# Seven block products over most of both wide layers' second matrix product, with weight sums made ahead in DRAM by adding transfers

## The chip, the core and the metric

One Trainium2 chip, one of its cores. The metric is device time of one execution in microseconds (us); lower is better. The kernel before ran three times at 1183.87, 1184.27 and 1186.08 us.

PE is the matrix engine (TensorE), PEld its weight loads, DVE VectorE, ACT ScalarE, POOL GpSimd, SP the engine that issues most transfers.

## The reference, cut to what matters

The input is 512 tokens of width 1024, float32. There are two layers. Each adds an attention part to the running sum `h` and then a wide layer (MLP) of width 4096:

```python
def sq_relu_mlp(h, w_up, w_down):
    u = jax.nn.relu(h @ w_up)
    return (u * u) @ w_down
...
    for layer in range(DEPTH):
        ...
        h = h + sq_relu_mlp(rmsnorm(h, norm_ffn[layer]), ffn_w_up[layer], ffn_w_down[layer])
    return rmsnorm(h, final_norm)
```

`w_up` is 1024x4096, `w_down` 4096x1024. The change is about the second product, `(u * u) @ w_down`, of both layers.

## The kernel before, in words

**Number format.** Every float32 operand is split into a high part (an ACT copy to float32r) and a low part (a DVE subtraction of the high part from the source); a product is three matrix instructions: high by high, high by low, low by high. Weights come in chunks: a transfer on SP's queue into a raw buffer, then the high part on ACT and the low part on DVE. `weights(i)` (L237) asks for the transfers of five chunks ahead and the splits of two chunks ahead; the split tiles `whi` and `wlo` have three buffers each.

**Plain products.** `product` (L415) with `mm3` (L500 to 503): for each 128 rows of the inner dimension and each 128 output columns, three matrix instructions over all 512 tokens, accumulating in a PSUM bank of its own; DVE adds the bank to `hT`, the running sum held transposed (L1265).

**Products with seven blocks.** `Seven` (L314) does a 2x2 block product (two 128-row blocks of the inner dimension, two 128-column blocks of the output, two halves of 256 tokens) with seven block products instead of eight. The sums of weight blocks are made after each load by three POOL instructions (`seven_chunk`, L302 to 304), the sums of token blocks by `sums` (L331). For 256 output columns `run` (L376) goes through all inner pairs, 21 matrix instructions over 256 tokens each (L388 to 390), and then combines the products in five ACT and DVE steps (L396 to 400).

**One wide layer**, `mlp` (L1250). The first product's first six tiles (of 128 columns of `u`) are made plainly (`plain`, L1160), the other 26 by `Seven`, two tiles in each of 13 runs of 84 matrix instructions. Each run squares its result (L1148, L1149) and either splits it into high and low parts (`pair_evac`) or keeps it raw (`raw_evac`). The second product is done in stages between those runs, as `SIZES` (L1108) says: layer 0 takes 6, 8 and 8 tiles of `u` plainly and 10 with `Seven`; layer 1 takes 6, 8 and 6 plainly, 8 with `Seven`, and 4 in a last product that puts tokens on the output's rows (`down`, L1621). While the last plain stage runs, `convert` (L1243) makes the token sums on DVE and splits them. Layer 0's second plain stage also carries the writing of the bias table for the next attention (`bias_rows`, L1215).

**Order of the work.** Each engine and each queue runs its own instructions in order; a scheduler orders them by readiness and program order, except where `keep_in_program_order` pins one and in the second attention, where the order is the written one (`fixed_order`, L957). 30 slots of 4 KB per partition (`Slot`) hold most intermediate tiles; they are handed out in rotation. A chunk of `Seven` takes a slot when more than `reserve` are free, else one of four `raw` buffers.

Attention comes first in each layer: layer 0 in `attend` (L961), where POOL scales each probability tile (L1005), layer 1 in `attend_C` (L1412; POOL at L1430), with plain products of later stages filled in (`Fill`, L471).

Of the kernel before, what the change touches and what calls it, by code (L numbers as in the profile page):

```python
# [16 lines left out]
S = 512  # L17
# [18 lines left out]
def encoder_kernel(ctx: ExitStack, tc: tile.TileContext, ins, out, dbg=None):  # L36
# [277 lines left out]
    class Seven:  # L314
# [61 lines left out]
        def run(self, ids, evac):  # L376
# [5 lines left out]
            for kp in range(self.np):  # L382
                hi, lo = weights(ids[kp])
                for n, ((a, b), (i, z)) in enumerate(zip(SEVEN, dst)):
# [5 lines left out]
                    PE.matmul(o, wl, x[:, 0], start=False, stop=kp == self.np - 1, skip_group_check=True)  # L390
                    yield 0.355
# [107 lines left out]

    def mm3(o, wh, wl, xh, xl, first, last):  # L500
        PE.matmul(o, wh, xh, start=first, stop=False)  # L501
        PE.matmul(o, wh, xl, start=False, stop=False)  # L502
        PE.matmul(o, wl, xh, start=False, stop=last)  # L503
# [271 lines left out]

    kst = Slot()
# [184 lines left out]
    def attend(heads, step):  # L961
# [46 lines left out]
        for h in heads:  # L1008
            for i in range(4):
                ripe = list(late_v)  # L1010
                p = scores(h, i)
# [77 lines left out]

    fill.add("z", product(w_in, 0, XP, tiles(768, 384), ev_cq, three))  # L1090
# [17 lines left out]
    SIZES = (6, 8, 8, 10), (6, 8, 6, 8, 4)  # L1108

    def first_product(l):  # L1110
# [10 lines left out]
        state = dict(c=SIZES[l][0], ids=None, plain=False, split=iter(()))  # L1121
# [68 lines left out]
        def stage(n, raw=0, more=0):  # L1190
# [4 lines left out]
            while left:  # L1195
                i = state["ids"]
                state["c"] += 2
                left -= 2
                if left:
                    ahead()  # L1200
                for _ in x7.run(i, raw_evac if more <= left < more + raw else pair_evac):
                    pass
# [12 lines left out]
    def bias_rows():  # L1215
        R, Fi, Fe = Slot(F32), Slot(F32), Slot(F32)
        rpb = ins["od_rpb"][0]
        for qr in range(8):
            SP.dma_start(R.t[16 * qr : 16 * qr + 16, 0:248],
                           rpb.rearrange("h a b -> h (a b)")[:, (7 - qr) * 31 : (7 - qr) * 31 + 248])  # L1220
# [9 lines left out]
        for c in range(16):  # L1230
            SP.dma_start(bxv[0, c].rearrange("r h k -> r h k"), Fi.t[:, (15 - c) * 8 : (15 - c) * 8 + 256])
# [3 lines left out]
            SP.dma_start(bxv[1, c][:, :, 128 * v : 128 * v + 128], Fe.t[:, off : off + 128])  # L1235
            yield
            SP.dma_start(bxv[1, c][:, :, 128 - 128 * v : 256 - 128 * v], Fe.t[:, 256:384])
# [5 lines left out]
    def convert(u7, R):  # L1243
        held = tc.keep_in_program_order
        for kp, raw in enumerate(R):
            yield from u7.sums(kp, raw, DVE, held)
            yield
            yield from u7.split(kp, held)

    def mlp(l, last=None):  # L1250

# [3 lines left out]
        beside = lambda m, i: None  # L1258
        k0 = 0
        for z, n in enumerate(SIZES[l][:3]):  # L1260
            U, R, V = stage(n, *(SIZES[l][3:] if z == 2 else ()))
            up = [s_.pair() for s_ in U]

            def ev(m, b):
                DVE.tensor_tensor(hT[:, m, :], hT[:, m, :], b, op=ALU.add)  # L1265

            gens = [product(w, k0, up, tiles(512 * c, 512), lambda j, b, c=c: ev(4 * c + j, b)) for c in range(2)]
            k0 += n
            work = iter(())
            if z == 2:  # L1270
                u7 = Seven(2 * len(R))
                ids = [u7.plan(w, 256 * m, k0) for m in range(4)]
                if last:
                    beside = last(k0 + 2 * len(R), V)
                reserve[0] = 8
                work = convert(u7, R)
            else:
                ahead()
            for c, gen in enumerate(gens):
                for i, _ in enumerate(gen):  # L1280
                    if z == 0:
                        later(c, i)
                    elif z == 1:
                        next(bias, None)
                    next(work, None)
            for _ in work:
# [442 lines left out]
```

## Time and profile before

| what | value |
|---|---|
| median of three runs | 1184.27 us |
| span of the profiled execution | 1184.0 us |
| PE matrix instructions | 7128, busy 98% of the span |
| DVE, ACT, POOL busy | 75%, 54%, 44% |
| bytes moved | 128.01 MB, mean 108 GB/s |

The page gives the profiled execution's span, from its first to its last instruction, and no other time of that execution; the median of the timed runs lies 0.27 us above it. Rows of a group of instructions give engine, operation, output and inputs, shape, count, busy time and mean duration, then the idle time of that engine just ahead of them and what ended it. Rows of a stretch give, for each engine, its busy time in that stretch and the number of instructions, then the granted PE clock, the DMA engines' busy share and GB/s. PE's busy time counts overlapping instructions as busy, so how fast PE goes is read from a stretch's length and its number of instructions.

### The profile page before, as it was taken

The page shows a single profiled execution, that of the slowest core. Times are in us where ns is not written, and L with a number is a line of the kernel's source. Part 1 is how long each engine was busy: PE and PEld are TensorE (multiplying, and loading weights), DVE is VectorE, ACT ScalarE, POOL GpSimd, SP SyncE. Part 2 cuts the span into 40 slices and gives each one's busy share as a digit, 9 for nine tenths or more (in the row PEclk, how much of TensorE's full clock was granted, in tenths as well). Part 3 has the DMA queues.
Part 4 walks back from the last instruction along what each step waited for, and adds up shares of the span by engine and source line. Part 5 has one row for each costly group of instructions (what it writes and reads, how often), then busy time and mean ns, then how long its engine had stood idle before and what let it go on. Part 6 is the DMA issues. An engine that isn't in the chain of part 4 may idle for free.

```text
span 1184.0 us, 19784 instructions
## 1 busy us (share of the span) xinstructions
PE 1160.5 (98%) x7128; PEld 1021.2 (86%) x7128; DVE 883.2 (75%) x1514; ACT 640.3 (54%) x1081; POOL 526.1 (44%) x662
## 2 busy tenths in 40 slices
PE   9989999999999999999999999999999999999997
PEld 8667778888899899988998998988889989998895
DVE  5788998878967368786884676667996736778975
ACT  4468676664546247562553565555554624666344
POOL 3267343224562377819602232231376625774710
PEclk9999999999999999999999999999999999999998
DMA  7223225212524723225226464433352341322412
GB/s 244 71 54 92 68 78 134 62 56 77 167 86 134 263 70 90 72 90 165 67 72 178 131 184 126 116 112 109 107 165 76 115 134 55 98 64 89 143 36 71
DMA packets 110145, 128.01 MB, mean 108 GB/s; under 512 B 9075, under 2 KB 86816, under 8 KB 110048
## 3 DMA queue, kind: packets, MB, share of 16 engines
q1 hardware_dynamic: 106992, 119.30, 33.5%
q0 software_dynamic: 2304, 6.31, 2.2%
q8 instruction: 56, 0.92, 0.3%
q10 hardware_dynamic: 752, 1.15, 0.3%
q14 instruction: 41, 0.34, 0.1%
HBM read 104.32 MB, written 6.29 MB: 93 GB/s over the span
## 4 chain that ended last, share of the span: by engine, by line
PE 81%; DVE 4%; ACT 1%; issue 1%; POOL 0%; DVEq 0%; ACTq 0%
PE mm L503 8%; PE mm L501 8%; PE mm L502 8%; PE mm L390 4%; PE mm L389 4%; PE mm L388 4%; PE t L388 3%; PE t L389 3%; PE t L390 3%; PE s L502 2%; PE s L503 2%; PE s L501 2%; PE s L390 2%; PE s L388 2%; PE s L389 2%; PE s L997 2%
## 5 line engine op out<-in xcount | busy, mean ns | idle before, releaser
L309 DVE TENSOR_TENSOR wlo<-a,whi 128x896 fp32r<-128x896 f32 x132 | 161.8, 1230 | 83.7 <-ACT whi L308 82.9
L308 ACT ACTIVATE whi<-a 128x896 fp32r<-128x896 f32 x132 | 125.0, 950 | 155.0 <-PE o L502 45.8
L501 PE MATMUL mm<-a,whi 128*128 128x512 f32 x485 | 195.9, 406 | 0.9 <-DVE a L915 0.7
L503 PE MATMUL mm<-a,wlo 128*128 128x512 f32 x485 | 192.1, 397 | 2.5 <-DVE wlo L202 2.5
L502 PE MATMUL mm<-a,whi 128*128 128x512 f32 x485 | 192.5, 397 | 0.1
L202 DVE TENSOR_TENSOR wlo<-raw,whi 128x1024 fp32r<-128x1024 f32 (+4 forms) x117 | 139.3, 1193 | 66.4 <-ACT whi L212 63.9
L212 ACT ACTIVATE whi<-raw 128x1024 fp32r<-128x1024 f32 (+3 forms) x120 | 116.4, 971 | 92.2 <-PE s L502 39.8
L302 POOL TENSOR_TENSOR a<-a 128x128 f32<-128x128 f32 x132 | 85.1, 645 | 173.3 <-DMA a<-in_ffn_w_up_dram 103.9
L303 POOL TENSOR_TENSOR a<-a 128x256 f32<-128x256 f32 x132 | 120.2, 910 | 10.3
L304 POOL TENSOR_TENSOR a<-a 128x128 f32<-128x128 f32 x132 | 115.1, 872 | 10.3
L503 PEld LDWEIGHTS mm<-a,wlo 128*128 128x128 f32 x485 | 91.7, 189 | 23.7 <-DVE wlo L202 3.4
L501 PEld LDWEIGHTS mm<-a,whi 128*128 128x128 f32 x485 | 91.8, 189 | 20.4 <-PE t L972 0.9
L502 PEld LDWEIGHTS mm<-a,whi 128*128 128x128 f32 x485 | 91.9, 190 | 17.4 <-DVE a L545 0.4
L388 PE MATMUL mm<-a,whi 128*128 128x256 f32 x370 | 103.9, 281 | 0.0
L389 PE MATMUL mm<-a,whi 128*128 128x256 f32 x370 | 103.9, 281 | 0.0
L390 PE MATMUL mm<-a,wlo 128*128 128x256 f32 x370 | 103.7, 280 | 0.0
L1005 POOL TENSOR_SCALAR p<-p,ti 128x512 f32<-128x512 f32 x64 | 46.2, 724 | 92.3 <-DVE ti L1004 81.1
L1430 POOL TENSOR_SCALAR p<-p,ti 128x256 f32<-128x256 f32 x64 | 35.6, 567 | 104.8 <-DVE ti L1429 91.8
L388 PE MATMUL t<-a,whi 128*128 128x256 f32 x264 | 74.2, 281 | 0.0
L389 PE MATMUL t<-a,whi 128*128 128x256 f32 x264 | 74.1, 281 | 0.0
L390 PE MATMUL t<-a,wlo 128*128 128x256 f32 x264 | 73.9, 280 | 0.0
L390 PEld LDWEIGHTS mm<-a,wlo 128*128 128x128 f32 x370 | 69.6, 188 | 0.2 <-DVE wlo L309 0.2
(338 smaller groups left out, 3210.8 us busy)
## 6 DMA issues: line engine op xcount, KB each, us to landing
a<-in_ffn_w_up_dram SPq DMA_DIRECT2D x104, 256.0 KB
raw<-in_ffn_w_down_dram SPq DMA_DIRECT2D x46, 512.0 KB
raw<-in_od_w_qkv_dram SPq DMA_DIRECT2D x64, 128.0 KB
a<-in_ffn_w_down_dram SPq DMA_DIRECT2D x28, 256.0 KB
raw<-in_ffn_w_up_dram SPq DMA_DIRECT2D x12, 512.0 KB
raw<-in_ev_w_in_dram SPq DMA_DIRECT2D x12, 384.0 KB
a<-a SPq DMA_DIRECT2D x18, 256.0 KB
bias<-bx SPq DMA_DIRECT2D x16, 256.0 KB
```

Source lines behind the costliest of these rows:

```text
L202: z = lambda: (eng or DVE).tensor_tensor(to, src, f32(high), op=ALU.subtract)
L212: ACT.activation(hi[:, 0:m], raw[:, 0:m], AF.Copy)
L303: POOL.tensor_tensor(r[:, 4:6], r[:, 2:3].to_broadcast([P, 2, P]), r[:, 0:7:6], op=ALU.add)
L304: POOL.tensor_tensor(r[:, 7], r[:, 3], r[:, 5], op=ALU.subtract)
L308: ACT.activation(hi[:, 0:896], raw[:, 128:1024], AF.Copy)
L309: DVE.tensor_tensor(lo[:, 0:896], raw[:, 128:1024], f32(hi[:, 0:896]), op=ALU.subtract)
L388: PE.matmul(o, wh, x[:, 0], start=kp == 0 and n in (0, 1, 3, 5), stop=False, skip_group_check=True)
L389: PE.matmul(o, wh, x[:, 1], start=False, stop=False, skip_group_check=True)
L390: PE.matmul(o, wl, x[:, 0], start=False, stop=kp == self.np - 1, skip_group_check=True)
L501: PE.matmul(o, wh, xh, start=first, stop=False)
L502: PE.matmul(o, wh, xl, start=False, stop=False)
L503: PE.matmul(o, wl, xh, start=False, stop=last)
```

## The change

- Layer 0's second product becomes 6 tiles of `u` plainly and 26 tiles (13 pairs) with seven block products; layer 1's becomes 6 plainly, 22 (11 pairs) with seven, and 4 in `down` as before. The 13 runs of the first product now follow one another, and their 26 tiles are all kept raw.
- The seven products use blocks of two 128-row blocks by two 512-column halves by two 256-token halves. The sums of weight blocks are made in DRAM, ahead of time: for each pair ACT issues two copies of 512 KB from `w_down` to a DRAM tile `made`, and POOL issues four transfers of 256 KB that add one block to another in DRAM. That makes 78 steps in layer 0 and 66 in layer 1. `tick` hands out one step for every 4.7 us (layer 0) or 5.5 us (layer 1) of counted PE work, from the start of the attention's filled products on; `drain` issues whatever is left before the sweeps.
- The products run in three sweeps over all pairs: two block products for each pair in the first sweep, two in the second, three in the third. A step loads its weights (512 KB, in the third sweep 768 KB) and splits them; the token sums and their splits are made one step ahead on DVE and ACT. Sums over products are partly left to PSUM: a bank goes on accumulating from one sweep into the next, and its content is added to or subtracted from `hT` in between. The last two pairs are done half by half of the output (`TAIL`).
- The bias table is written beside the second and third sweeps, and layer 1's first four groups of transposes of `hT` move from beside `Seven` into `down`.

```diff
+    def tick(us):
+        beat["left"] -= us
+        if beat["left"] <= 0:
+            beat["left"] += beat["every"]
+            next(beat["work"], None)
...
     def mm3(o, wh, wl, xh, xl, first, last):
+        tick(MM3)
...
+    FIRST, RAW, MORE = 6, (26, 22), (0, 4)
+    class SumsAhead:
+        def add(self, kp, to, src, of=None):
+            tc.keep_in_program_order(POOL.dma_start(self.block(kp, *to), self.block(kp, *src, of), accum_op=ALU.add))
+        def steps(self):
+            for kp in range(self.n + 3):
+                if kp < self.n:
+                    for z in range(2):
+                        tc.keep_in_program_order(ACT.dma_start(self.made[kp, z], self.w[kp, z]))
+                        yield
+                for back, to, src, of in ((1, (1, 1), (0, 1), self.w), (1, (0, 1), (0, 0), self.w),
+                                          (2, (0, 0), (1, 1), None), (3, (1, 0), (0, 0), None)):
+                    if 0 <= kp - back < self.n:
+                        self.add(kp - back, to, src, of)
+                        yield
...
+        def tokens(self, kind, kp):
+            if kind == 0:
+                split_to(d[:, :, 0], d[:, :, 1], r[:, 0:4:2])
+                self.one(kp)
+                if kp < 2:
+                    self.two(kp)
+            elif kind == 1:
+                for q, src in enumerate((r[:, 0], s2)):
+                    split_to(d[:, q, 0], d[:, q, 1], src)
+                if kp + 2 < self.n:
+                    self.two(kp + 2)
+                if kp + 2 >= self.n:
+                    self.three(kp + 2 - self.n)
+                    self.four(kp + 2 - self.n)
+            else:
+                if kp + 2 < self.n:
+                    self.three(kp + 2)
+                    self.four(kp + 2)
+                split_to(d[:, :, 0], d[:, :, 1], r[:, 1:3])
+                one = pp.tile([P, 512], F32R, tag="p", name=nm("u"))
+                e = one.rearrange("p (z n) -> p z n", z=2)
+                split_to(e[:, 0], e[:, 1], r[:, 3])
...
+            PRODUCTS = [
+                [(X, 0, at(0)), (Z, 1, at(S))],
+                [(Y, 0, at(S)), (X, 1, at(0))],
+                [(Y, 2, at(S)), (Z, 1, lambda h, m: (h[2].t[:, 0:S], h[2].t[:, S:], P * m)), (X, 0, at(0))],
+            ]
...
+                if kp == self.n - 1:
+                    with tc.high_priority():
+                        for z in range(2):
+                            if kind == 0:
+                                add(z, 0, 0, X)
+                            else:
+                                add(z, 1, 1, Y, ALU.subtract)
+                                add(z, 0, 1, X)
...
-        for z, n in enumerate(SIZES[l][:3]):
-            U, R, V = stage(n, *(SIZES[l][3:] if z == 2 else ()))
...
+        U = stage(FIRST)[0]
...
+        R = stage(0, RAW[l] + MORE[l], 0, lambda: sweeps.append(Sweeps(w, FIRST, made)))[1]
...
+        drain()
+        reserve[0] = 6
+        beside = last(FIRST + RAW[l], V) if last else lambda kind, kp: None
+        for n, (kind, kp) in enumerate(sweeps[0].run(R)):
...
+    ahead0, ahead1 = (SumsAhead(ins["ffn_w_down"][l], FIRST, RAW[l] // 2) for l in range(2))
+    beat.update(every=4.7, work=ahead0.steps())
...
+    beat.update(every=5.5, work=ahead1.steps())
```

`one` to `four` are single DVE additions or subtractions of 128x256; `split_to` is an ACT copy and a DVE subtraction; `add` is a DVE addition or subtraction of a 128x512 PSUM bank to `hT`, sixteen of them in a layer's sweeps. In a step of the first and the second sweep PE does 24 matrix instructions over 256 tokens, in one of the third 36.

More of the change, by code (lines that the diff above doesn't have):

```diff
@@ L1188, in ahead, with stage @@
             state["ids"] = x7.plan(w, P * state["c"])
-        def stage(n, raw=0, more=0):
+        def stage(n, raw=0, more=0, then=lambda: None):
             if not state["plain"]:
@@ L1257, in mlp @@
         bias = bias_rows() if l == 0 else iter(())
-        beside = lambda m, i: None
-        k0 = 0
-        for z, n in enumerate(SIZES[l][:3]):
-            U, R, V = stage(n, *(SIZES[l][3:] if z == 2 else ()))
[L1262 to L1286, printed above, removed]
-                pass
-            reserve[0] = 1
-            for s_ in U:
-                s_.free()
```

220 lines of the change are left out of this document (193 added, 27 removed).

## The prediction

> **What bounds the kernel now.** I read the page first: busy shares, the granted clock, the chain that ended last.
>
> ```profile
> span 1184.0 us, 19784 instructions
> ...
> PE 1160.5 (98%) x7128; PEld 1021.2 (86%) x7128; DVE 883.2 (75%) x1514; ACT 640.3 (54%) x1081; POOL 526.1 (44%) x662
> ...
> PEclk9999999999999999999999999999999999999998
> ...
> PE 81%; DVE 4%; ACT 1%; issue 1%; POOL 0%; DVEq 0%; ACTq 0%
> ```
>
> PE is busy 98% of the span at full clock, and 81% of the chain runs on it. A busy PE need not be at its peak, so next I cut the two wide layers into stretches, one for each product, and divided by the instructions that the code issues in each.
>
> ```profile
> core 0: us, PE busy (x) PEld busy (x) DVE busy (x) ACT busy (x) POOL busy (x), PEclk, DMA share, GB/s
> 375.90:420.50 44.60, 44.60 (x194) 36.08 (x193) 20.12 (x23) 11.32 (x12) 18.30 (x31) 1.00 0.72 237
> 420.50:510.45 89.95, 89.94 (x757) 89.52 (x756) 67.66 (x77) 58.67 (x76) 63.78 (x77) 1.00 0.25 73
> 510.45:554.85 44.40, 44.40 (x194) 36.09 (x193) 37.94 (x55) 17.61 (x24) 23.54 (x31) 1.00 0.44 140
> 554.85:604.45 49.60, 49.60 (x421) 49.58 (x420) 41.14 (x48) 27.07 (x36) 26.31 (x30) 1.00 0.22 66
> 617.30:838.00 220.70, 220.06 (x1284) 191.50 (x1282) 149.04 (x371) 121.32 (x269) 54.78 (x99) 1.00 0.47 131
> 938.10:982.60 44.50, 44.50 (x194) 36.10 (x193) 20.68 (x24) 11.45 (x13) 15.50 (x21) 1.00 0.41 131
> 982.60:1071.95 89.35, 89.35 (x757) 89.31 (x756) 68.20 (x76) 57.93 (x73) 60.39 (x75) 1.00 0.27 78
> 1071.95:1109.30 37.35, 35.12 (x146) 28.20 (x145) 33.81 (x47) 15.49 (x23) 23.33 (x27) 0.95 0.36 111
> 1109.30:1150.70 41.40, 41.40 (x352) 41.35 (x352) 32.13 (x36) 18.89 (x24) 15.57 (x20) 1.00 0.24 77
> ```
>
> Rows 1, 3 and 6 are the plain stages of eight tiles (8 x 8 x 3 = 192 instructions over 512 tokens): 0.232 us each. Rows 2, 4 and 7 are work with seven blocks: 89.35 / 756 = 0.1182 us for 256 tokens, so an instruction over half the tokens takes 0.51 of one over all. Seven block products for eight therefore cost 0.875 x 2 x 0.1182 / 0.232 = 0.892 of the plain product. PE goes at these rates without gaps in every stretch but the sixth tile stage of layer 1 (1071.95 to 1109.30): 144 instructions x 0.232 = 33.4 us, but 37.35 passed.
>
> Why there, two more cuts and PE's waits show:
>
> ```profile
> 1085.00:1095.00 10.00, 10.00 (x45) 8.16 (x44) 10.00 (x17) 3.48 (x5) 5.19 (x6) 1.00 0.17 52
> 1100.00:1105.00 5.00, 2.77 (x8) 1.94 (x7) 5.00 (x6) 1.47 (x2) 4.69 (x7) 0.76 0.50 158
> ...
> PE mm L503 <- DVE wlo L202: 2.5, 2, 2.2
> ```
>
> DVE, which makes the token sums there beside the weight splits, is busy without a gap; PE waits 2.2 us for it and then gets a lower clock: 2.2 of waiting cost 37.35 - 33.4 = 4.0 us. DVE's share of that stage is 33.81 / 37.35 = 0.905. In layer 0's stage (510.45 to 554.85) it is 0.854, and PE lost nothing.
>
> **What PE saves.** Layer 0: the two plain stages and the `Seven` stage take 44.60 + 44.40 + 49.60 = 138.6 us. The sweeps are 13 pairs x 7 blocks x 4 x 3 = 1092 instructions at 0.1182 = 129.1. Saved: 9.5 us. Layer 1: 44.50 + 37.35 + 41.40 = 123.25. The last row holds 336 + 16 instructions; the 16 are the transposes that move to the last product and still cost 41.40 - 39.7 = 1.7. The sweeps are 11 x 84 = 924, 109.2 us, and with the transposes 110.9. Saved: 12.3, of which 4.0 is the stage with the stall, which goes. The first product, attention and `down` keep their PE instructions. Together 21.8 us. The span of 1184.0 and what lies around it (0.3, going by the median of 1184.27) gives 1184.3; less 21.8 is 1162.5 with nothing on the other side.
>
> **DVE in the sweeps: the term that decides.** POOL's weight sums go, but the splits do not, and the token sums now come just in time, beside them.
>
> ```profile
> 601.64 1.22 DVE L202 TENSOR_TENSOR wlo<-raw,whi 128x1024 fp32r<-128x1024 f32 x1
> ...
> L202 DVE TENSOR_TENSOR wlo<-raw,whi 128x1024 fp32r<-128x1024 f32 x88 | 113.2, 1288 | 55.7 <-ACT whi L212 53.4 <-PE o L390 2.2
> L363 DVE TENSOR_TENSOR a<-a,a 128x512 fp32r<-128x512 f32 x51 | 41.2, 846 | 0.7 <-ACT a L362 0.7
> L1265 DVE TENSOR_TENSOR hT<-hT,mm 128x512 f32<-128x512 f32 x18 | 12.0, 680 | 2.2 <-PE mm L503 2.1
> L363 DVE TENSOR_TENSOR a<-a,a 128x256 fp32r<-128x256 f32 x17 | 9.7, 573 | 0.0
> L338 DVE TENSOR_TENSOR a<-a,a 128x256 f32<-128x256 f32 x9 | 4.0, 442 | 0.0
> ```
>
> The first row is one split with POOL quiet (layer 0's end). For the same shapes the groups with POOL's sums beside them are longer: 1288, 846 and 573 ns against 1220, 680 and 442. In the sweeps POOL has no sums, so I take 1.22, 0.68 and 0.44. For each pair: first sweep 1.22 + 0.68 + 0.44 = 2.34 (PE 24 x 0.1182 = 2.84); second 1.22 + 3 x 0.44 = 2.54 (PE 2.84); third 1.22 + 2 x 0.68 + 3 x 0.44 = 3.90 (PE 36 x 0.1182 = 4.25). That is 8.78 for PE's 9.93. Sixteen additions to `hT` are 10.9 a layer. Layer 0: 13 x 8.78 + 10.9 = 125.0 of 129.1 (0.97). Layer 1: 11 x 8.78 + 10.9 + 2.7 for the four extra splits = 110.2 of 109.2 (1.01). DVE is thus at PE's own length, above the 0.905 at which PE waited. Splits run two steps ahead and absorb the 2.7 us bursts of additions between sweeps, but little more. Bounds for a layer: nothing (as at 0.854), and the 4.0 of the stage at 0.905. I take 2 for layer 0 and 3 for layer 1, since both lie nearer the stalled stage and layer 1 is over PE's length. 5.0 us.
>
> The Trainium skill (TensorE: Matmul & The Clock Gate, Part 1) has the clock halved only after an idle window of about 3.4 us. The wait of 2.2 us above was followed by a clock of 0.76, so this trace does not bear that out, and I go by the trace. By the page the upper bound would be 2.2 instead of 4.0, and with the terms scaled the time 2.2 us less.
>
> **POOL beside the first product.** The 13 runs now follow one another, 129.2 us (1092 x 0.1182), with 52 chunks to sum and, at one add for 7.05 us (two steps in three at 4.7), 18 adds in layer 0; in layer 1, at 8.25 us, 16.
>
> ```profile
> L303 POOL TENSOR_TENSOR a<-a 128x256 f32<-128x256 f32 x17 | 15.9, 937 | 1.3
> L304 POOL TENSOR_TENSOR a<-a 128x128 f32<-128x128 f32 x18 | 15.4, 853 | 1.4
> L302 POOL TENSOR_TENSOR a<-a 128x128 f32<-128x128 f32 x18 | 12.8, 711 | 14.6 <-PE s L389 10.1 <-DMA a<-in_ffn_w_up_dram 4.5
> ...
> L1338 POOL DMA_DIRECT2D a<-a x16: 517/525/640, 628.2 to 772.7; - x16
> L1610 ACTq DMA_DIRECT2D out_dram<-a x4: 546/554/655, 1171.8 to 1179.0; - x4
> ```
>
> The first three rows are from 1010 to 1070: 44.1 us for 18 chunks, 2.45 each, where PE takes 21 x 0.1182 = 2.48. Nine runs in a row already keep PE at 0.1182, and POOL stood idle for 14.6 of those 60 us, mostly for a free buffer. 52 x 2.45 + 18 x 0.525 = 136.9 against 129.2 plus what POOL is ahead at the start. In the 60 us PE used 24 chunks while POOL made 18, so it was at least six (15 us) ahead, without the slots that split tiles took then. I put it at 0. Bounds: nothing, and 136.9 - 129.2 = 7.7 a layer if it had no lead.
>
> **Issues beside attention.** By the ticks 173 us of counted work are attention in layer 0 and 163 in layer 1: 37 and 30 steps, so 44 adds and 22 copies; the rest fall beside the first product and its plain stage. An add holds POOL 0.525 us, with the scaling of probabilities (L1005, L1430) queued behind it, for which PE's transposes wait. A copy holds ACT 0.554, with exponentials and splits behind it. In full that is 44 x 0.525 + 22 x 0.554 = 35.3 us.
>
> ```profile
> POOL p L1430 <- DVE ti L1429: 91.8, 27, 6.6
> ...
> PE t L1452 <- POOL p L1430: 0.2, 1, 0.2
> ```
>
> POOL itself waits 91.8 us for DVE in the second attention, and PE waited 0.2 us for POOL's scaling, once in 64; filled products cover the delay. If that cover went, the 35.3 us would show. Bounds: nothing and 35.3; near the first, I take 1.5.
>
> **Entry, exit, transfers.** The first tokens of a sweep may be queued behind the combining of the last run.
>
> ```profile
> L396 ACT ACTIVATE a<-mm 128x256 f32<-128x256 f32 x18 | 6.5, 364 | 0.0
> ...
> L362 ACT ACTIVATE a<-a 128x512 fp32r<-128x512 f32 x51 | 31.6, 626 | 41.5 <-DVE a L340 11.4 <-DVE a L336 10.7 <-POOL a L340 6.6
> ```
>
> That chain is 0.36 + 3 x 0.68 + 0.44 = 2.84, then 0.63 + 0.68 for the split: 4.2 us a layer at most. The first pair's raw tile is finished 12 runs earlier, so its split can go ahead; I take 0.5 a layer, 1.0. At the exit the next layer's splits cover the last additions; 0. Loads in the sweeps are 1.75 MiB in 9.93 us, 185 GB/s; the stage at 375.90 moved 237 at a share of 0.72, so this is 0.56. The bias table, which moves from that stage to the last two sweeps of layer 0 (and there stands on SP's queue between weight loads), made it 0.72 instead of the 0.41 of its twin at 938.10: 0.31 x 44.6 = 13.8 us, over 92 us another 0.15. The sum, 0.71, is what the stage at 375.90 carried without loss; 0. Copies and adds are 2 MiB in 28.2 us, a share of 0.23 if a byte counts once, 0.56 if every read and write does (5 MiB); on the 0.47 of the second attention that is at most 1.0, and with its 33 us a group 0.95. 0.
>
> Sum: 1162.5 + 5.0 + 0 + 1.5 + 1.0 = **1170.0 us**.
>
> **Rivals.** *DVE sets the pace of the sweeps* (slower). Place: second and third sweep. If DVE takes what it takes beside POOL's sums (1.29, 0.85, 0.57), or loses as much between its instructions to waits for ACT's high parts, a pair costs 2.71 + 3.00 + 4.70 = 10.41 for PE's 9.93: 13 x 10.41 + 10.9 = 146.2 and 11 x 10.41 + 10.9 + 3.4 = 128.8, over PE by 36.7. Time: 1162.5 + 36.7 + 2.5 = 1201.7. It decides from where DVE exceeds PE's 238.3 by 21.8 - 2.5 = 19.3, at 257.6, 9.5% more than the 235.2 above. For it: the shares of 0.97 and 1.01, and the stall at 0.905. Against: POOL's only work there is four short instructions of the bias table, and ACT's splits are 5376 columns a pair, at 0.63 us for 512 some 6.6 us of 9.93. 0.15.
>
> *The issues show in attention* (a smaller gain or none). At a third of 35.3, 11.8 us: 1162.5 + 6.0 + 11.8 = 1180.3; it eats the gain at (21.8 - 6.0) / 35.3 = 0.45. For it: in the second attention the order is written out, so a late instruction cannot be passed. Against: the 0.2 us. The Trainium skill (DMA: Bandwidth & Descriptors, Specifications) gives about 1 us until the first byte of a transfer that POOL issues, for its descriptors; were that POOL's time, the full price would be 56 us, but 0.525 is what its rows show. 0.15, half of it still faster, half within 0.2%.
>
> *The sums are not there in time* (the change doesn't do what it says). 78 x 4.7 = 367 us of steps stand against 368 of counted work before the sweeps, 66 x 5.5 = 363 against 358, and the second sweep begins 13 x 2.84 = 37 us later, with loads asked for 14 us ahead. Were an add 8 us for the queue instead of 7.05, layer 0's last would be 52 x 0.95 = 49 us late, 26 more than those 23: 1162.5 + 7.5 + 26 = 1196. Nothing in the trace shows an add; plain transfers of POOL show no such length of issue. 0.05.
>
> **The numbers.** 0.65 for the forecast with its own range 1161.5 to 1177 (low: none of the terms, and 0.0005 us in the pace over 2016 instructions; high: 4.0 a layer for DVE, 4.2 for an entry, a few us of the issues). With the second rival that makes 0.80, up to where its gain is gone: 1161.5 to 1186.5. Faster by over 0.2% (2.4 us, about what a measurement of this kernel can tell from no change): 0.65 + 0.08 = 0.73. Within 0.2%: 0.07. Slower: 0.15 + 0.05 = 0.20.
>
> **What would show it.** Right: 180 fewer instruction-equivalents of 256 tokens and sweeps of about 131 and 112 us; DVE above 0.93 of them with PE waits for `wlo` or token splits of a few us, in the second and third sweep; 13 runs at 0.1182 with POOL near 0.95 busy; attention as long as before within 2 us. Wrong: PE waiting for DVE over more than 10 us in a sweep (first rival); stretches of attention longer by over 5 us with waits for POOL's `p` (second); SP or PE waiting for `made` (third); or the 13 runs slower than 0.121.

## The result and the profile after

The changed kernel takes 1198.38 us (median of four runs, 1197.39 to 1199.76), the kernel before on the same chip 1184.92: a ratio of 1.0113 with a 95% interval of 1.0098 to 1.0127. It is 13.5 us slower; the forecast was 14 us faster. The profiled execution took 1199.76 us.

The page after, the lines that answer to those of before:

```profile
span 1197.9 us, 21331 instructions
...
PE 1152.0 (96%) x7668; PEld 1040.3 (87%) x7668; DVE 905.0 (76%) x1627; ACT 675.5 (56%) x1157; POOL 527.5 (44%) x650
...
PEclk9998999999999998998999999999999999999999
...
PE 64%; POOL 12%; DVE 10%; DMA 5%; issue 4%; ACT 3%; SPq 1%; ACTq 0%; POOLq 0%; DVEq 0%
```

PE carried 81% of the chain before and carries 64% now; POOL and DVE have a tenth each, and DMA, which the chain did not name, has 5%. The busy shares hardly moved (POOL 44% in both): what was lost does not show in them, so the next view is the table of stretches. First before, for two stretches not yet shown (from the first move of a finished q tile on SP's queue to the first run of the first product; and from the end of layer 0's wide layer to layer 1's first run):

```profile
83.40:336.20 252.80, 248.55 (x1336) 203.63 (x1335) 216.17 (x434) 162.19 (x320) 113.24 (x130) 1.00 0.33 94
604.60:898.50 293.90, 293.26 (x1658) 253.32 (x1657) 210.49 (x463) 151.57 (x316) 96.42 (x142) 1.00 0.47 134
```

And after: attention 0, runs 0, sweeps 0, attention 1, runs 1, sweeps 1, end:

```profile
83.20:347.50 264.30, 252.59 (x1331) 207.23 (x1332) 216.52 (x435) 164.01 (x326) 131.36 (x155) 0.98 0.60 151
347.50:485.70 138.20, 132.74 (x1094) 131.84 (x1093) 97.13 (x115) 81.15 (x100) 117.62 (x148) 0.98 0.63 152
485.70:625.20 139.50, 132.39 (x1096) 131.29 (x1095) 107.42 (x177) 74.80 (x116) 18.10 (x4) 0.98 0.63 200
625.20:921.00 295.80, 293.64 (x1656) 252.68 (x1656) 218.74 (x468) 154.52 (x321) 112.21 (x161) 1.00 0.69 180
921.00:1052.80 131.80, 129.89 (x1094) 129.03 (x1094) 94.93 (x110) 79.71 (x97) 116.64 (x148) 1.00 0.62 152
1052.80:1162.90 110.10, 109.68 (x927) 109.38 (x926) 94.59 (x158) 63.46 (x99) 0.00 (x0) 1.00 0.56 185
1162.90:1197.90 35.00, 26.12 (x129) 20.87 (x127) 19.27 (x45) 17.24 (x36) 0.00 (x0) 0.93 0.20 61
```

The reader is to compare lengths. With the stretch edges that the prediction quotes (layer 0's wide layer 336.2 to 604.6, layer 1's 898.5 to 1150.7):

| stretch, us | before | after | difference | the prediction's own terms |
|---|---|---|---|---|
| up to the first move of q | 83.4 | 83.2 | -0.2 | 0 |
| rest of attention 0 | 252.8 | 264.3 | +11.5 | 1.5 for both attentions |
| layer 0's wide layer | 268.4 | 277.7 | +9.3 | -9.5 + 2 + 0.5 = -7.0 |
| attention 1 | 293.9 | 295.8 | +1.9 | in the 1.5 |
| layer 1's wide layer and the end | 285.5 | 276.9 | -8.6 | -12.3 + 3 + 0.5 = -8.8 |

The differences add up to 13.9, the difference of the two spans. Layer 1 came out as forecast, by luck: its sweeps took 110.1 us where the sum had 109.2 + 3 + 0.5, and its 13 runs took 131.8 instead of 129.2, so two errors of 2.6 us cancel. The losses are in layer 0: the attention, whose own work the change leaves as it was (A), the 13 runs at 138.2 instead of 129.2 (B), the sweeps at 139.5, where PE's instructions alone are 129.1 (C). One reading of each follows from the trace, and the experiments test them.

**A.** SP's queue, before and after, around the first two q tiles (L635 to 637 before are L649 to 651 after; columns: start, length, engine, line):

```profile
83.42 0.50 SPq L635 DMA_DIRECT2D a<-a  x1
84.82 0.50 SPq L636 DMA_DIRECT2D a<-sc  x1
85.64 0.46 SPq L637 DMA_DIRECT2D a<-sc  x1
```

```profile
83.16 0.50 SPq L649 DMA_DIRECT2D a<-a  x1
84.57 0.50 SPq L650 DMA_DIRECT2D a<-sc  x1
87.67 0.46 SPq L651 DMA_DIRECT2D a<-sc  x1
```

The third move overwrites what the first one reads, so it goes when the first has landed: 2.2 us after it before, 4.5 us now. The chain of waits after has both:

```profile
83.16 4.49 DMA a<-a
87.67 4.42 DMA a<-sc
```

The scores of the next heads wait for the last move, and the delay adds up: the second tile's first move stands at 109.2 us instead of 101.4, the third's at 133.4 instead of 121.5. By the third tile the whole loss of A is there. Besides the moves a weight load (`raw<-in_ev_b_w_ukv_dram`, 3.31 us) stands on that chain; how the delay divides between it and the moves is open.

**B.** POOL in layer 0's runs, after (L302 to 304 make one chunk's weight sums, L803 is an add):

```profile
437.50 0.80 POOL L803 DMA_DIRECT2D made<-in_ffn_w_down_dram  x1
438.06 0.72 POOL L302 TENSOR_TENSOR a<-a 128x128 f32<-128x128 f32 x1
...
440.83 0.47 POOL L302 TENSOR_TENSOR a<-a 128x128 f32<-128x128 f32 x1
...
443.32 0.81 POOL L803 DMA_DIRECT2D made<-made x1
448.84 0.81 POOL L803 DMA_DIRECT2D made<-made x1 [4.71 <-DMA made<-made]
```

POOL has no gap until 443.3; then it waits 4.71 us for a chained add to land. PE stalls for 4.4 us soon after. Two readings: that wait, or a POOL that is short of time anyway.

**C.** SP and POOL in layer 0's sweeps, after:

```profile
527.53 0.35 SPq L1306 DMA_DIRECT2D a<-in_ffn_w_down_dram  x1
544.84 0.72 SPq L1276 DMA_DIRECT2D bx<-a  x1
...
547.02 1.82 SPq L1304 DMA_DIRECT2D a<-made  x4
```

```profile
517.62 0.41 POOL L1267 MEMSET a<- 128x376 f32 x1 [40.76 <-DVE wlo L1311]
...
527.97 16.84 POOL L1270 COPY a<-a 128x128 f32<-128x128 f32 x1 [9.69 <-DMA a<-in_od_rpb_dram]
544.76 0.65 POOL L1271 COPY a<-a 128x248 f32<-128x248 f32 x1
```

A copy of the bias table that takes 0.45 us in the kernel before takes 16.84 here. The first transfer of the table (L1276) is pinned on SP's queue and waits for it, and the sweep's weight loads (L1304) stand behind it: SP issues nothing for 17 us. The stretch ahead, that of just these 17 us, and the one after:

```profile
505.00:527.90 22.90, 22.77 (x194) 22.57 (x193) 22.90 (x46) 12.17 (x21) 0.66 (x2) 1.00 0.42 133
527.90:544.80 16.90, 16.90 (x145) 16.90 (x145) 16.64 (x35) 10.65 (x21) 16.83 (x2) 1.00 0.05 16
544.80:570.00 25.20, 19.30 (x143) 18.60 (x142) 10.34 (x12) 9.65 (x13) 0.61 (x2) 0.86 0.80 255
```

In the 17 us PE runs on what was loaded, DVE is busy 16.64 of 16.90 us, and the DMA engines stand at a share of 0.05; then the loads come late, PE is busy 19.3 of 25.2 us and its clock is 0.86.

**What the stalls cost twice.** The granted clock was at half in four stretches of the changed kernel's A, B and C:

```profile
90.30:97.10 6.80, 4.97 (x20) 4.50 (x20) 3.16 (x7) 1.77 (x4) 1.48 (x3) 0.50 0.28 72
117.60:121.00 3.40, 3.40 (x14) 2.81 (x13) 3.21 (x8) 2.52 (x6) 3.15 (x4) 0.50 1.04 252
452.10:458.90 6.80, 6.02 (x26) 5.72 (x27) 4.23 (x5) 2.51 (x4) 6.41 (x9) 0.50 0.41 81
551.10:557.90 6.80, 4.21 (x18) 3.92 (x19) 1.48 (x2) 1.97 (x3) 0.00 (x0) 0.50 0.92 313
```

Ahead of each lie 3.4 us in which PE was busy for 0 to 1.2 us. Half the clock for 10.2 us in A, 6.8 in B and 6.8 in C is worth 5.1, 3.4 and 3.4 us (an estimate). With PE's longest waits (6.5 us for `a<-sc` in A; 5.4 in B and 7.0 in C for the splits, and for `hT` in C) that makes 11.6, 8.8 and 10.4, about the three losses. In the kernel before, the clock was at half only once between the first move of q and the end of layer 1's wide layer, from 1102.6 to 1106.0, in the stage whose stall the prediction describes.

### The profile page after: what moved, and what is told of

Its sections match the earlier page's. It is cut to its first block, busy times and chain, and to the rows that moved or that the text cites. A ratio compares the mean times of both kernels' runs of the same rounds, so it can differ in the third digit from the quotient of the medians.

```text
span 1197.9 us, 21331 instructions
## 1 busy us (share of the span) xinstructions
PE 1152.0 (96%) x7668; PEld 1040.3 (87%) x7668; DVE 905.0 (76%) x1627; ACT 675.5 (56%) x1157; POOL 527.5 (44%) x650
## 4 chain that ended last, share of the span: by engine, by line
PE 64%; POOL 12%; DVE 10%; DMA 5%; issue 4%; ACT 3%; SPq 1%; ACTq 0%; POOLq 0%; DVEq 0%
PE mm L515 6%; PE mm L517 6%; PE mm L516 6%; POOL a L303 4%; POOL a L304 3%; PE s L1038 2%; POOL a L302 2%; PE t L1414 2%; PE t L1413 2%; PE t L1415 2%; PE o L1026 2%; PE t L1013 2%; POOL a L1270 1%; DMA raw<-in_ffn_w_down_dram 1%; PE s L516 1%
## 5 line engine op out<-in xcount | busy, mean ns | idle before, releaser
L309 DVE TENSOR_TENSOR wlo<-a,whi 128x896 fp32r<-128x896 f32 x98 | 121.5, 1241 | 72.9 <-ACT whi L308 66.8
L515 PE MATMUL mm<-a,whi 128*128 128x512 f32 x395 | 160.0, 407 | 0.6 <-DVE sc L922 0.3
L517 PE MATMUL mm<-a,wlo 128*128 128x512 f32 x395 | 156.2, 396 | 0.4 <-DVE wlo L202 0.3
L516 PE MATMUL mm<-a,whi 128*128 128x512 f32 x395 | 156.2, 395 | 0.1
L202 DVE TENSOR_TENSOR wlo<-raw,whi 128x1024 fp32r<-128x1024 f32 (+4 forms) x87 | 100.7, 1162 | 32.1 <-ACT whi L212 32.0
L212 ACT ACTIVATE whi<-raw 128x1024 fp32r<-128x1024 f32 (+3 forms) x90 | 84.4, 942 | 66.1 <-PE s L516 13.6
L517 PEld LDWEIGHTS mm<-a,wlo 128*128 128x128 f32 x395 | 74.4, 189 | 17.4 <-DVE wlo L202 1.3
L515 PEld LDWEIGHTS mm<-a,whi 128*128 128x128 f32 x395 | 74.4, 189 | 16.4 <-issue 1.1
L304 POOL TENSOR_TENSOR a<-a 128x128 f32<-128x128 f32 x98 | 84.2, 859 | 7.7
L302 POOL TENSOR_TENSOR a<-a 128x128 f32<-128x128 f32 x98 | 67.6, 690 | 44.6 <-DMA a<-in_ffn_w_up_dram 31.3
L516 PEld LDWEIGHTS mm<-a,whi 128*128 128x128 f32 x395 | 74.6, 189 | 13.5 <-DVE a L559 0.4
L388 PE MATMUL mm<-a,whi 128*128 128x256 f32 x280 | 79.7, 285 | 4.5 <-ACT whi L308 4.4
L1311 DVE TENSOR_TENSOR wlo<-a,whi 128x1024 fp32r<-128x1024 f32 x51 | 62.3, 1223 | 24.9 <-ACT whi L1310 24.8
L389 PE MATMUL mm<-a,whi 128*128 128x256 f32 x280 | 79.4, 284 | 0.0
```

The lines of the kernel that those rows point to most:

```text
L202: z = lambda: (eng or DVE).tensor_tensor(to, src, f32(high), op=ALU.subtract)
L302: POOL.tensor_tensor(r[:, 6], r[:, 0], r[:, 1], op=ALU.subtract)
L304: POOL.tensor_tensor(r[:, 7], r[:, 3], r[:, 5], op=ALU.subtract)
L309: DVE.tensor_tensor(lo[:, 0:896], raw[:, 128:1024], f32(hi[:, 0:896]), op=ALU.subtract)
```

## The experiments

All stretches below are of one profiled execution each; the times are medians, with the ratio to the kernel before on the same chip. "A" is the stretch from the first move of q to the runs. Edges of stretches are read to about 0.2 us.

| kernel | A | runs 0 | sweeps 0 | attention 1 | runs 1 | sweeps 1 | time, us | ratio (95%) |
|---|---|---|---|---|---|---|---|---|
| before | 252.8 | | | 293.9 | | | 1184.9 | |
| after | 264.3 | 138.2 | 139.5 | 295.8 | 131.8 | 110.1 | 1198.4 | 1.0113 (1.0098 to 1.0127) |
| e1 | 261.0 | 136.2 | 130.3 | 296.1 | 132.1 | 110.1 | 1189.0 | 1.0056 (1.0034 to 1.0078) |
| e2 | 258.0 | 129.2 | 138.8 | 295.3 | 128.8 | 109.6 | 1179.4 | 0.9970 (0.9956 to 0.9984) |
| e3 | 252.8 | 134.3 | 139.4 | 295.3 | 128.9 | 110.1 | 1178.6 | 0.9960 (0.9948 to 0.9973) |
| e4 | 266.6 | 136.2 | 137.9 | 294.8 | 132.0 | 110.2 | 1199.0 | 1.0125 (1.0104 to 1.0146) |
| e5 | 253.5 | 131.2 | 140.0 | 294.0 | 129.2 | 109.3 | 1179.1 | 0.9963 (0.9951 to 0.9976) |
| e7 | 252.7 | 135.4 | 132.2 | 297.3 | 132.3 | 110.1 | 1178.3 | 0.9949 (0.9935 to 0.9963) |
| e8 | 261.2 | 137.7 | 129.4 | 295.9 | 131.9 | 110.2 | 1188.6 | 1.0037 (1.0024 to 1.0049) |
| e9 | 257.1 | 140.7 | 129.4 | 295.7 | 129.4 | 110.1 | 1181.6 | 0.9973 (0.9957 to 0.9988) |
| e10 | 252.2 | 129.2 | 129.2 | 293.9 | 130.1 | 110.2 | 1173.2 | 0.9907 (0.9894 to 0.9921) |
| e11 | 252.6 | 134.3 | 130.2 | 295.7 | 129.3 | 110.3 | 1171.4 | 0.9892 (0.9878 to 0.9907) |
| e12 | 258.0 | 129.2 | 139.6 | 297.6 | 128.8 | 112.8 | 1186.8 | 1.0027 (1.0012 to 1.0042) |
| e13 | 253.8 | 129.9 | 135.3 | 294.3 | 128.8 | 109.3 | 1170.2 | 0.9880 (0.9849 to 0.9910) |

Kernels whose program is the same up to a point still differ there: A of `after`, e1, e8 and e12 is 264.3, 261.0, 261.2 and 258.0. A single A can thus be off by several us while copies and adds run beside it. The clock has a part in that: in A it was at half for 10.2 us in `after`, 6.8 in e8 and not at all in e12. The kernels that have no steps beside the moves of q and one for 3.7 or 3.85 us later (e3, e7, e10, e11, e13) lie between 252.2 and 253.8.

**e1: the table made early.**

```diff
+                if c == 0 and i < 12:
+                    next(bias, None)
```

> Reading of the trace after, three causes. A: heads A of the first attention are 11 us longer, because the moves of q on SP's queue take 4.4 us instead of 2.2 while copies and adds use the same 16 DMA engines. B: layer 0's 13 runs take 138 us instead of 129, because POOL, with 0.8 us for each add, loses its lead and then waits 4.7 us for a chained add. C: layer 0's sweeps take 139.3 us instead of 129, because POOL's copy of the bias table takes 16.8 us beside a DVE that never pauses, and SP holds the weight loads behind a bias transfer that waits for that copy. This kernel moves the loads of the bias table, its memsets and POOL's two copies into layer 0's first plain stage; the 48 transfers stay in the sweeps. By C: sweeps of layer 0 129 to 132 us, SP without the gap of 17 us, the whole about 1189 (7 to 10 less than 1198.4). Rival C2, the 48 small transfers themselves hold up the weight loads: sweeps 136 to 139, the whole 1195 to 1198. Rival C3, the forecast's rival that DVE sets the pace: sweeps 139, the whole 1198, DVE busy throughout.

Sweeps 130.3, the whole 1189.0: both as C says. The 48 small transfers are still there and cost nothing, so C2 falls. DVE's work in the sweeps is still there, so C3, the forecast's own rival, falls too.

**e8: the same place, another engine.**

```diff
-        POOL.tensor_copy(Fe.t[:, 0:248]..., rv)
+        ACT.activation(Fe.t[:, 0:248]..., rv, AF.Copy)
```

(and the same for `Fi`)

> The two copies of the bias table stay at their place in the sweeps, but ScalarE makes them instead of POOL; the memsets stay on POOL. By C (the copy on POOL is starved beside DVE): sweeps of layer 0 129 to 133 us, nearly the 130.3 of the kernel with the table made early; the whole 1188 to 1190. Rival: the place is what costs (loads of the table, the wait for a free slot, the transfers behind them on SP's queue), whichever engine copies: 137 to 140, the whole 1196 to 1199.

Sweeps 129.4, the whole 1188.6. ScalarE's copy and the whole sweeps of e8:

```profile
524.52 0.44 ACT L1270 ACTIVATE a<-a 128x128 f32<-128x128 f32 x1
```

```profile
482.10:611.50 129.40, 129.40 (x1096) 129.26 (x1095) 107.39 (x177) 76.53 (x118) 0.66 (x2) 1.00 0.67 217
```

0.44 us instead of 16.84 at the same place, and PE without a gap. So the place was not at fault, nor the transfers, but POOL's copy beside DVE. POOL's memset of 128x376, which reads nothing, took 0.41 us in the changed kernel ten us earlier, beside a DVE that was busy 22.90 of 22.90 us. The Trainium skill (SBUF — State Buffer, Who interferes with whom) says that a DVE instruction with two inputs in SBUF contends with a POOL instruction that reads SBUF and not with one that only writes there, and that one of the two blocks fully. These rows agree: 16.84 against 0.41. That the shared port is the cause is the page's statement; the runs show only which engine's copy starves.

**e3: no steps beside the moves of q.**

```diff
+        if n == 24:
+            beat.update(every=3.85, work=ahead0.steps())
...
-    beat.update(every=4.7, work=ahead0.steps())
```

> Layer 0's copies and adds begin 24 steps into the first attention, one for each 3.85 us of counted work instead of 4.7 from the start, so that the first three quarters of heads A have none. By A: the stretch up to the 13 runs 336 to 339 us instead of 347.5. By B, with adds denser beside the runs: 138 to 145 there. Sweeps 139 as before. The whole 1188 to 1195. Rival, the 11 us belong to the issues and not to the moves of q: they come back in the later steps, with waits for POOL's scaling, and the stretch is 343 or more.

A is 252.8, what it was before, although the same steps now stand closer together in the rest of that stretch:

```profile
83.10:335.90 252.80, 248.77 (x1336) 203.42 (x1335) 217.95 (x434) 161.43 (x320) 128.27 (x151) 1.00 0.61 156
```

The DMA share of 0.61 here, without loss, is that of the changed kernel (0.60), with a loss of 11.5. The mean share says nothing; what counts is what runs while a short transfer is on the chain. The runs did not get longer as expected: they take 134.3 us, 4 less than in the changed kernel, although 23 adds stand beside them instead of 20. The whole is below its expected range.

**e2 and e5: which part of a step costs.** e2 has `pass` in place of the adding transfer. In e5 copies and adds take 64 of each 512 columns:

```diff
-            ... self.block(kp, *to), self.block(kp, *src, of), accum_op=ALU.add
+            ... self.block(kp, *to)[:, 0:64], self.block(kp, *src, of)[:, 0:64], accum_op=ALU.add
```

> Leaves out the adding DMAs, so that the weight sums are not made; copies, loads and everything else stay. By B: the 13 runs 129 to 131 us (138 before), layer 1's 129 to 130 (131.6). By A: the copies are 2 of the 5 MiB that a group reads and writes, so the first attention keeps 3 to 6 of its 11 us. C is untouched: sweeps of layer 0 139. The whole 1179 to 1184. Rival A2, it is the engine time of the issues: if ACT's copies, all 11 us stay (1186); if POOL's adds, none (1174 to 1176). Rival B2, the 13 runs are late for slow weight loads beside the copies' traffic and not for POOL: they stay at 134 to 138.

> Same copies and adds, in number, engine and order, each over an eighth of the columns; the sweeps read the unsummed weights, so the weight sums are left out. By A (traffic): moves of q near 2.2 us, the stretch up to the 13 runs 336 to 340. Rival A2 (time of the issues): 346 to 348. For B: if the landing of chained adds makes POOL wait, small adds land sooner and the runs take 129 to 133 us; if POOL's time for an add is enough, with 0.8 us each still, they stay at 135 to 138. Sweeps of layer 0 139 by C. The whole 1179 to 1189.

e2: A keeps 5.2 of its 11.5 us, the runs are at 129.2 and 128.8, the whole 1179.4. The 5.2 lies in the expected 3 to 6, but e12, whose program is the changed kernel's up to the runs, has the same 258.0, so e2 does not show what the adds' share of A is. e5: with every issue in place and an eighth of the bytes, A loses 0.7. So A is bytes on the DMA engines, not the engine time of issues (A2 falls). The moves themselves say the same. From a tile's first move to its third the kernel before takes 2.2 us, three times over. The first tile's takes 4.0 to 5.0 us in each kernel with whole copies beside it (`after`, e1, e2, e4, e8, e12), e2 without adds among them, and 2.2 or 2.3 in all others; e5 has 2.3, 3.5 and 2.2 for its three tiles. For B, e5 seemed to speak for the landing of the adds: POOL's add lasts as long as before (0.81 to 0.86 us in the rows), and the runs take 131.2.

**e4: the chained wait taken away.**

```diff
-                                          (2, (0, 0), (1, 1), None), (3, (1, 0), (0, 0), None)):
+                                          (3, (0, 0), (1, 1), None), (5, (1, 0), (0, 0), None)):
```

> The chained adds stand 3 and 5 groups behind the copy instead of 2 and 3, with the start, the pace and the number of adds as they are. By B (POOL waits for the landing of a chained add): no wait of POOL for made from made above 1 us, layer 0's 13 runs 129 to 133 us instead of 138.4, layer 1's 129 instead of 131.9. Rival B2, POOL's own time for the adds uses up its lead: 136 to 139. The first attention (11 us) and the sweeps of layer 0 (139) as in the changed kernel. The whole 1188 to 1192, by the rival 1196 to 1199.

POOL's longest wait for a transfer is now 1.7 us, for a copy, and the runs are still at 136.2 and 132.0; the whole 1199.0. So my reading of B is not the whole cause, and B2 stands: POOL's time. To see it, count in the trace how long before PE's first use POOL had finished a chunk's sums (layer 0, us):

| kernel | adds beside the runs | 3rd chunk | 19th | 35th | 51st | runs 0 |
|---|---|---|---|---|---|---|
| after | 20 | 21.6 | 19.4 | 11.2 | 9.1 | 138.2 |
| e3 | 23 | 20.6 | 16.8 | 10.4 | 8.5 | 134.3 |
| e4 | 22 | 21.3 | 18.2 | 10.9 | 8.5 | 136.2 |
| e5 | 20 | 29.0 | 22.2 | 15.8 | 8.5 | 131.2 |
| e13, below | 16 | 22.4 | 18.4 | 13.8 | 8.6 | 129.9 |
| e10, below | 14 | 22.1 | 21.1 | 16.8 | 13.5 | 129.2 |
| e12, below | 8 | 22.9 | 19.5 | 18.3 | 14.6 | 129.2 |
| e2, no adds | 0 | 25.8 | 24.6 | 23.1 | 16.3 | 129.2 |

In `after`, e3, e4 and e5, PE loses time in the middle of the runs once the lead is down to some 10 to 13 us; e13 goes down to 11 there and loses 0.8 us in all. The splits that follow need only 2.2 of these (0.95 on ACT and 1.24 on DVE). The rest shows in the order of the records: between the 24th and the 45th chunk of `after`, e3 and e4, ACT's split of a chunk never begins before POOL has finished the sums three chunks on, and often 0.03 us behind them. Three chunks of 2.5 us and the two splits make 9.7 us, an estimate of the lead that cannot be spent. `weights` asks for loads and sums five chunks ahead and for splits two ahead, the same distance of three; what holds ACT to it no run shows. The changed kernel enters with 21 and has some 10 to spend; twenty adds at 0.57 us are 11.4. e5 enters with 29, and so gets nearly through. That its smaller transfers give it the larger lead (weight loads arriving sooner) is likely, but no run isolates it.

The wait for the chained add has a part too. Short of time alone, POOL costs 5 us in e3 and 7 in e4, in waits of PE of less than 1 us each. In the changed kernel the wait of 4.7 us came when no lead was left, PE stalled for 4.4 us, and the clock was at half behind that: 9.0 with fewer adds. In e10 POOL waits 1.4 us for a chained add and 3.0 for a copy while it is 14 us ahead, and PE goes on.

**e12: few steps beside the runs.** With ScalarE's copies as in e8:

```diff
+        beat["every"] = (20.0, 20.0)[l]
         R = stage(0, RAW[l] + MORE[l], 0, ...
...
-        drain()
+        beat.update(left=0.0, every=(2.5, 2.5)[l])
...
             beside(kind, kp)
+            tick(0.355)
```

> ScalarE copies the table, as in an earlier kernel (1188.6: 344.5 up to the runs, 137.7 runs, 129.4 sweeps; 131.9 runs in layer 1); beside the 13 and 11 runs there is a step only each 20 us of counted work, and the rest follow in the sweeps, one for 2.5 us. Theory B as the runs so far leave it: POOL enters the runs about 20 us ahead, 10 us is the least at which PE does not wait, and adds take more than the 10 us between. With a third of them: runs 131 to 133 us in layer 0 and 129 in layer 1, the whole 1179 to 1184. Rival: the chunks alone are too slow for POOL with a head start of 20 us: runs 136 or more. Rival: the rest of the transfers is now felt in the first sweep: sweeps 133 or more, with SP or PE waiting for made.

Runs at 129.2 and 128.8 (13 in each layer) with eight adds beside layer 0's instead of twenty: B is POOL's budget. The second rival is true as well: the remaining transfers, pressed into the sweeps, cost 10.2 and 2.6 us there against e8, where 8.5 and 3.1 were saved in the runs.

```profile
343.90:473.10 129.20, 129.20 (x1095) 129.20 (x1094) 100.47 (x115) 81.19 (x100) 110.25 (x136) 1.00 0.44 118
472.90:612.60 139.70, 134.61 (x1096) 133.71 (x1095) 107.13 (x177) 75.53 (x118) 9.77 (x13) 0.96 0.81 239
```

The sweeps with a DMA share of 0.81 lose 10 us, with ACT and PE waiting for loads; with 0.67 (e8) they lose nothing.

**e7 and e9: three mends together.** e1, e3 and e4 in one; e9 with a step for each 3.0 us.

> The table made early, the steps begun 24 steps into the attention at one for 3.85 us, and the chained adds at 3 and 5 groups, together. If A, B and C are the whole loss and independent: up to the runs 336, runs 129 to 131, sweeps 130.3, between the layers 295, runs 129, sweeps 110, the end 34.8, together 1164 to 1167. If the spread chain does nothing: runs 134, the whole 1169 to 1171. If the gains do not add up, for example because table and adds meet on POOL: above 1172.

> As the one before, with a step for each 3.0 us, so that fewer adds stand beside the 13 runs and more beside the rest of the attention. If adds beside the runs still cost: 1 to 3 us less than that kernel. If the traffic shows in heads B and the next products as it did in heads A: the stretch up to the runs 338 to 342 and the whole 2 to 5 us more.

Neither reaches its first case: e7 takes 1178.3, e9 1181.6, and the runs are at 135.4 and 140.7. Spreading the chain had not helped POOL in e4. Making the table early brings a stall of its own: in e1, e7 and e9 PE waits 1.5 to 5.7 us for ACT's split some 14 to 18 us into the runs, and ACT waits 7 to 11 us for POOL's sums of one chunk. In these three kernels 11 of the chunks summed in the runs lie in the `raw` buffers, in the others one or none. That the table's three slots, held until its last transfer, bring this about is likely, but no run isolates it. In e9 the denser steps cost A 4.3 us, as its second case had it. Of the 33 us that the losses come to in the changed kernel (A 11.5, B 9.0 and 2.6, C 10.3), e7 gets 20 back.

**e11: the two mends that stood, e3 and e8.**

> Layer 0's steps begin 24 steps into the attention at one for 3.85 us, and ScalarE copies the bias table; the chain of adds is as in the changed kernel. From the stages of the two kernels with one of these each: 336 up to the runs, 134.3 runs, 129.4 sweeps, 295.3 between, 129 to 132 runs, 110 sweeps, 34.8 the end: 1168.8 to 1172. If A and C were not independent: above 1174.

1171.4, and from the first move of q on every stretch lies within 1 us of what was put together from the two. A and C are independent.

**e10 and e13: all of it.** e10 is e11 with ten steps beside the program's first products, and one step for 12 and 10 us beside the runs and for 3.5 and 3.0 in the sweeps. e13 leaves the early steps out (7 and 9 beside the runs, 4.0 and 3.5 in the sweeps).

> ScalarE copies the table; some ten steps of layer 0 stand beside the first products of the program, none beside the moves of q, the others from 24 steps into the attention at 3.7 us; beside the runs one for 12 and 10 us, the rest in the sweeps, one for 3.5 and 3.0. If A, B and C are the whole loss: up to the runs 336, runs 130 to 132, sweeps 129.5, between 295.3, runs 129, sweeps 110, the end 34.8: 1164 to 1167. If the early steps delay the first products or the moves of q: 340 or more up to the runs and 1169 or more.

> ScalarE copies the table; layer 0's steps begin 24 steps into the attention, one for 3.7 us and none ahead of that; beside the runs one for 7 us in layer 0 and 9 in layer 1, the rest in the sweeps at 4.0 and 3.5 us. Up to the runs 334 to 336, runs 130 to 132 (134.3 with a step for each 3.85 us), sweeps 129.5 to 131, between 295.3, runs 129 to 130, sweeps 110, the end 34.8: 1164 to 1168. If a first sweep with steps is disturbed as it was with one step for 2.5 us (139.6): 1171 or more.

In e10 the runs and the sweeps of layer 0 are both at 129.2, so B and C are gone together; but the first move of q comes at 92.1 instead of 83.4, with one wait of PE of 4.0 us for weights while the early copies run, and that is its second case (1173.2 where 1169 or more was said). The other kernels have that move at 80.6 to 87.2. e13 has the runs at 129.9, and its sweeps at 135.3 are halfway to its own rival. At 1170.2 it is as fast as e11 within the intervals, and both beat the kernel before by 1.1 to 1.2%. The 1164 us at which all three would be free was not reached.

```profile
344.40:473.50 129.10, 129.10 (x1094) 129.10 (x1093) 99.97 (x115) 81.02 (x100) 113.35 (x142) 1.00 0.52 134
473.40:602.70 129.30, 129.30 (x1096) 129.30 (x1095) 107.08 (x177) 76.05 (x118) 2.08 (x4) 1.00 0.72 230
```

## Why the prediction was wrong, point by point

- **What PE saves: right.** e10 has 129.1 and 129.3 us for 1092 instructions each, the 129.1 of the prediction. The saving is there; the steps that pay for it were mis-costed.
- **"DVE in the sweeps: the term that decides": too large, and it did not decide.** Forecast 2 and 3 us; measured 0.3 (e8, 129.4 for 129.1) and 0.9 (110.1 for 109.2). DVE was put at 0.97 and 1.01 of PE's time, and was busy 107.4 of 129.4 (0.83) and 94.6 of 110.1 us (0.86). The durations were right. One part of the error can be read from these rows of layer 1's sweeps after (busy time, then the mean):

```profile
L1311 DVE TENSOR_TENSOR wlo<-a,whi 128x1024 fp32r<-128x1024 f32 x24 | 29.3, 1224 | 8.6 <-ACT whi L1310 8.6
L1359 DVE TENSOR_TENSOR a<-a,a 128x256 fp32r<-128x256 f32 x22 | 8.3, 422 | 0.0
```

  22 of 0.422 are 9.3, but the engine was busy 8.3 us with them: short instructions overlap in the records. Number times mean is too much for them. Over all DVE rows of layer 1's sweeps the durations add up to 106.6 us and the busy time is 94.6, so overlap makes some 12 of the 15.6 us between the forecast 110.2 and the busy time; the rest was not divided up. The first rival had chance 0.15 for a time of 1201.7, near to what came, but by a mechanism that was not at work: PE waited 0.4 us for DVE in layer 1's sweeps.
- **"Issues beside attention", 1.5 us, with the transfers of copies and adds put at 0: the step that failed first (A, +11.5; attention 1 +1.9, where the kernels lie between 293.9 and 297.6).** It priced each step by the engine that issues it, and looked for who waits behind that engine. e5 shows that this part was right: with all issues and an eighth of the bytes, A is 0.7 us longer. The transfer itself had been dealt with as a mean share of the DMA engines, "at most 1.0", and put at 0. What counted was how long a short transfer on the chain takes while long ones are under way: 4.5 us instead of 2.2, two such in a row for a q tile, and then a lower clock.
- **"POOL beside the first product", put at 0 (B, +9.0 and +2.6).** The mechanism was named and the bounds were given (0 to 7.7 a layer), but the lead of 15 us was counted as if all of it could be spent. The lead was 21, and some 10 of it could not be spent, since ACT's splits kept three chunks behind POOL. An add's price was right: 0.57 us until POOL's next instruction, for the 0.525 of the row it was taken from. The sum of 52 chunks and 18 adds, 136.9, stands close to the 138.2 that the runs took, and to the 136.2 of e4, but that is partly luck: POOL made 43 of the 52 in that stretch, and 3.4 us of the loss are the clock's. The value was near the upper bound, not at 0. The sign named for it did show: 138.2 / 1092 = 0.127 us, slower than 0.121.
- **"The bias table ... 0" (C, +10).** It was weighed as bytes (0.15 of DMA share), and the first rival's counter-argument called its POOL work "four short instructions". One of these was not short: beside a DVE that never pauses, POOL's copy took 16.84 us, and what was queued behind it on SP's pinned queue were the weight loads of the sweep. The prediction had noted that the table stands between weight loads there, and gave no price for a blocked queue.
- **"The issues show in attention" and "the sums are not there in time".** Neither happened. PE's largest waits in A are for `a<-sc` (6.5 us), and none is for POOL's `p`; the sums were there. The long stretch of attention was named as a sign of the second rival, and it came from another cause.

## What to carry to other kernels

Price a transfer that is added beside other work three ways: the time of the engine that issues it, its share of the DMA engines, and what it does to the shortest transfer on the chain in that stretch; a mean share of 0.6 cost nothing in one place and 11 us in another. When a step moves on a pinned queue, ask what each instruction ahead of it waits for, and whether an engine beside it is now busy without a pause. A lead of one engine over another can be spent only down to the distance that the stages between them keep; read that distance from the records, since here it was some four times the 2.2 us that the stages' own work takes.

## What the runs showed of the hardware that was not expected

- POOL's copy of 128x128 within SBUF: 0.45 us in the kernel before, 16.84 beside DVE's unbroken two-input additions and subtractions; the same copy on ScalarE 0.44, POOL's memset there 0.41.
- An adding transfer of 256 KB in DRAM: 0.57 us from its start to POOL's next instruction (437.50 to 438.06; the record itself says 0.80), and a median of 5.2 us (`made` from `made`) from issue to landing; with an eighth of the bytes 2.9 us, and the same time on POOL.
- A move within SBUF of half a tile's rows: 2.2 us until the move that waits for it went, with the DMA engines at a share of 0.33 over the stretch; 4.5 us while copies and adds ran (3.0 to 5.0 over the tiles of the kernels with whole copies there).
- The granted clock was at half for 3.4 or 6.8 us at a time, behind 3.4 us in which PE had been busy for 0 to 1.2 us, and not only behind stalls that long: in the kernel before a wait of 2.2 us was enough.
